# A transformer block whose pools hand out their SBUF rooms in a new order

## The chip, the cores and the metric

The kernel runs on one core of a Trainium2 chip. The metric is device time in microseconds (us) of one execution; lower is better. The program on the core is five instruction streams: TensorE (PE; its weight loads are listed apart as PEld), VectorE (DVE), ScalarE (ACT), GpSimd (POOL) and SyncE (SP). Nearly all DMAs are issued by SP, one after the other, and each stream runs in its own order and waits on semaphores for the others.

## The reference, cut to what matters

One layer on 1024 rows of width 1024, in float32: a mixer of two kinds of attention, then cross-attention to a memory of 256 rows, then a squared-ReLU MLP. The change lies in the projection ahead of the mixer.

```python
def reference(x, mem, norm1_g, w_in, ...):
    x = x + _hybrid_mixer(_rms_norm(x, norm1_g), w_in, ...)
    x = x + _memory_xattn(_rms_norm(x, norm2_g), mem, ...)
    x = x + _sq_relu_mlp(_rms_norm(x, norm3_g), w_ff_in, w_ff_out)
    return x

def _hybrid_mixer(h, w_in, ...):
    c_q, c_kv, k_idx, w_idx, q_nsa, kv_nsa, g_nsa = split(h @ w_in)     # the projection
    q_d = rope(rms_norm(rms_norm(c_q) @ w_dsa_uq))                     # 8 heads of 64
    k_d, v_d = split(rms_norm(c_kv) @ w_dsa_ukv)
    q_i = rope(rms_norm(c_q) @ w_idx_q)                                # picks 256 keys per row
    ...
    return o @ w_out                                                   # o: both attentions

def _rms_norm(x, g):
    return x * rsqrt(mean(x * x) + EPS) * g
```

## The kernel before, in words

Rows go in tiles of 128, so there are eight row tiles. `build` first runs `project(p1, 0)`, the projection of row tiles 0 to 3, on its own; its tiles live in the pool `p1`. Then `p1` is closed, and two streams run interleaved through `together`: `attend`, the attention of all row tiles (pool `aw`), and `fill`, which is `project(p2, 1)` (row tiles 4 to 7, pool `p2`), then `memory` (cross-attention's keys and values, pool `dn`), then output projections and MLP. After that a tail follows with pools of its own. PE gets dense matmuls from `fill` and many small ones from `attend`.

**Pools.** A pool hands out rooms in SBUF in the order in which its tags are first asked for; `RINGS` says how many rooms a tag has. `reuse_waits="tile"` makes a tile of a later pool wait only for the old tiles whose addresses it covers. `p2` lies where `p1` lay, and `aw` begins inside it too. Before, the order in `p2` is: `xh` (the scaled rows of the second half), `c8` (3 rooms: two for `KT`, the raw keys that `compress` reads, and one for `cq`), `c4`, `kraw`, `pc`, then the weights `wlo` and `whi`. So the second half's first weights lie on `p1`'s `whi` and `wlo`, which the last matmuls of the first half still read. The rooms `qin` and `qta` of attention's first tiles lie on `p1`'s `relu` and `c8`.

**Order.** `tc` is opened with `schedule_with_timeline_sim`: the order of each engine's stream is set by a planner which takes the waits (the rooms' too) into account, not by the order of the code alone. Moving a room can therefore move instructions.

**Names.** `weights` (L308) loads `w_in` in chunks of 256 columns, two row blocks of 128 at a time; in the second half the matmuls are plain float32 and the loads go straight into rooms called `wlo` and `whi` in turn (SP, L277), four loads to a chunk. `gemm` (L322) multiplies them; its matmuls all have line L223, as `mm` records them. `project` (L393) scales the rows (L408 in the second half, on DVE), loads eleven small vectors and tables into `pc` (L424 to L434, SP), and hands the results on: `stage_q` writes query tiles into `st` and stores them to DRAM (`q<-st`, L446). Attention reads them back (`qin<-q`, L603), turns them (L610 to L623) and transposes them on PE (`psPT<-c_ident,qd`, L629). `row_scales` (L387) makes the sums of squares of row tiles 4 to 7 (`squares` in `x4`, `relu`, then a matmul with `ones` and the square root), in the first half's `project`. In `memory`, `memT` is loaded (L908), squared on ACT (L374), reduced on DVE (L376), summed over partitions on PE (`psM<-ones,relu`) and scaled (L911).

Of the kernel before, what the change touches and what calls it, by code (L numbers as in the profile page):

```python
# [9 lines left out]
F32 = mybir.dt.float32  # L10
F32R = mybir.dt.float32r
# [11 lines left out]
P = 128  # L23
L = 1024
DM = 1024
# [9 lines left out]
NS = 4  # L35
G = 2
RINGS = {
    "p1": {"x4": 5, "st": 2, "relu": 4, "wraw": 4, "whi": 6, "wlo": 6, "c8": 4, "c4": 2, "kraw": 5, "pc": 2},
    "p2": {"x4": 5, "st": 1, "relu": 2, "whi": 4, "wlo": 4, "c8": 3, "c4": 1, "kraw": 4, "pc": 2},
    "dn": {"b4": 4, "h": 8, "relu": 2, "wraw": 2, "whi": 4, "wlo": 4},  # L40
    "res": {"b4": 4, "g": 2},
    "d2": {"b4": 2, "h": 8, "relu": 2, "whi": 4, "wlo": 4},
# [99 lines left out]
def chain(*gens):  # L142
    for x in gens:
        yield from x


def alternate(*streams):
    streams = list(streams)
    i = 0
    while streams:  # L150
        i %= len(streams)
        w = next(streams[i], None)
        if w is None:
            streams.pop(i)
        else:
            i += 1
            yield w
# [12 lines left out]
def build(nc, tc, I, C, out):  # L170
    v, s, g, te = nc.vector, nc.scalar, nc.gpsimd, nc.tensor
    ctx = ExitStack()
    W = {n: I[n][0] for n in _INS}
# [9 lines left out]
    p1 = p1_pool.__enter__()  # L183
# [6 lines left out]
    def ring(pool, tag, shape, dt=F32):  # L190
        n = RINGS[pool.name if isinstance(pool.name, str) else "dn"][tag]
        return pool.tile(shape, dt, tag=tag, name=tag, bufs=n)
# [29 lines left out]
    def mm(o, a, b, start, stop):  # L222
        te.matmul(o, a, b, start=start, stop=stop)  # L223
# [84 lines left out]
    def weights(pool, xs, nk, wsrc, parts):  # L308

        w = sum(n for _, n in parts)  # L310
        for k0 in range(0, nk, KG):
            kn = min(KG, nk - k0)
            srcs, o = [], 0
            for c0, n in parts:
                srcs.append((lambda r, o=o, n=n: r[:, :, o:o + n],
                             wsrc[k0 * P:(k0 + kn) * P, c0:c0 + n].rearrange("(k p) n -> p k n", p=P)))
                o += n
            ws = load_w(pool, [P, kn, w], *srcs) if len(xs) == 2 else load_whole(pool, [P, kn, w], *srcs)
            for k in range(kn):
                yield [x[:, k, :] for x in ws]  # L320

    def gemm(pool, xs, nk, nt, wsrc, chunks, consume, begun=None):  # L322

        for ci, parts in enumerate(chunks):
            w = sum(n for _, n in parts)
            gr = begun if ci == 0 and begun else list(weights(pool, xs, nk, wsrc, parts))
            for t in range(nt):
                pt = pst(TAGS[pool.name][0], [P, w])
                for k in range(nk):
                    if len(xs) == 1:  # L330
                        mm(pt, xs[0](t, k), gr[k][0], k == 0, k == nk - 1)
                        continue
                    wh, wl = gr[k]
                    xh, xl = xs[0](t, k), xs[1](t, k)
                    mm(pt, xh, wh, k == 0, False)
                    mm(pt, xh, wl, False, False)
                    mm(pt, xl, wh, False, k == nk - 1)
                consume(ci, t, pt)
                yield nk * (5 - len(xs)) * w / 2400.0

    def xT(pool, nt, whole=False):

        parts = [pool.tile([P, DM // P, nt * P], F32 if whole else F32R, tag="x" + n, name="x" + n)
                 for n in ("h" if whole else "hl")]
        return (parts, [lambda t, k, x=x: x[:, k, t * P:(t + 1) * P] for x in parts],
                lambda t: [x[:, :, t * P:(t + 1) * P] for x in parts])
# [20 lines left out]
    def load_xT(T):  # L367

        late["xT"][T] = small(srow, "S", L, bufs=NS).rearrange("p (k c) -> p k c", c=P)
        return nc.sync.dma_start(late["xT"][T], I["xT"][T].rearrange("p (k c) -> p k c", c=P))  # L370
# [7 lines left out]
        mm(pt, part, ones, True, True)  # L378
        return rsqrt_of(pool, pt, DM, 1, tag, r)

    def row_scale(pool, T):

        squares = ring(pool, "x4", [P, DM // P, P])
        norm_scale(pool, late["xT"][T], squares, st["r"][:, T:T + 1], "n")
        v.tensor_scalar(st["rn"][:, T:T + 1], st["r"][:, T:T + 1], -1.0, None, op0=ALU.mult)

    def row_scales(pool):  # L387

        for T in range(4, NT):
            row_scale(pool, T)  # L390
            yield 1.0

    def project(pool, part, late, st):  # L393
        t0, nt = PARTS[part]
        whole = part > 0
        parts, xf, xt_of = xT(pool, nt, whole)
        begun = []
        if not whole:
            load_xT(0)
            ws = weights(pool, xf, DM // P, W["w_in"], [(968, 256)])  # L400
            for t in range(1, nt):
                begun += [next(ws) for _ in range(KG)]
                load_xT(t)
            begun += list(ws)
        for t in range(nt):
            raw, g1 = late["xT"][t0 + t], gT["norm1_gT"]
            if whole:
                v.tensor_tensor(xt_of(t)[0], raw, g1[:, :, None].to_broadcast([P, DM // P, P]), op=ALU.mult)  # L408
            else:
                hi, lo = xt_of(t)  # L410
                for k in range(DM // P):
                    s.activation(hi[:, k, :], raw[:, k, :], AF.Copy, scale=g1[:, k:k + 1])
                    v.scalar_tensor_tensor(lo[:, k, :], raw[:, k, :], g1[:, k:k + 1], hi[:, k, :],
                                           op0=ALU.mult, op1=ALU.subtract)
                row_scale(pool, t)
            yield 1.0
        pe = late["pe"]
        cq = [ring(pool, "c8", [P, nt, 2, P], F32 if whole else F32R) for _ in xf]
        ckv = [ring(pool, "c4", [P, nt, P], F32 if whole else F32R) for _ in xf]
        kraw = [ring(pool, "kraw", [P, 6, 64]) for t in range(nt)]  # L420
        KT = []
        pc = ring(pool, "pc", [P, 512])
        cqg, ckvg, ctab = pc[:, 0:256], pc[:, 256:384], pc[:, 384:512].rearrange("p (a d) -> p a d", d=64)
        nc.sync.dma_start(cqg, row(W["dsa_cq_g"]).to_broadcast([P, 256]))  # L424
# [65 lines left out]
        def w_in(chunks, first, begun=None):  # L490
            return gemm(pool, xf, DM // P, nt, W["w_in"], chunks,
                        lambda ci, t, pt: consume(ci + first, t, pt), begun)
# [31 lines left out]
                    tc.keep_in_program_order(load_xT(4 + u))  # L524
                yield 1.0

        KT += [ring(pool, "c8", [P, 2, nt * P + (0 if part else 16)]) for _ in range(2)]
        for kv in range(0 if part else 2):
            p3 = pe[:, kv, :].rearrange("p (a l) -> p a l", a=2)
            g.tensor_copy(KT[kv][0:64, :, nt * P:], p3[0:64])  # L530
# [4 lines left out]
        yield from (alternate if part == 0 else chain)(*pair_)  # L535
        yield from gemm(pool, [lambda t, k, c=c: c[:, t, :] for c in ckv], 1, nt,
                        W["w_dsa_ukv"], [[(0, 128)]], consume_kv)
        yield from alternate(w_in([[(456, 256)], [(712, 256)]], 2), k_prep())
        ups = chain(*[gemm(pool, [lambda t, k, c=c: c[:, t, k, :] for c in cq], 2, nt,
                           W[name], [[(0, 256)], [(256, 256)]],  # L540
                           lambda ci, t, pt, k=k: stage_q(k, ci, t, pt)) for k, name in ((0, "w_dsa_uq"), (2, "w_idx_q"))])
        yield from ups if whole else alternate(ups, row_scales(pool))

    def compress(pool, part, KT, pe, st, ctab):
        t0, nt = PARTS[part]
# [803 lines left out]
```

## Time and profile before

| | us |
|---|---|
| median of 3 runs | 1786.45 (1784.96 to 1792.77) |
| the profiled execution, its time | 1783.33 |
| its span, first to last instruction | 1781.6 |

| engine | busy share of the span |
|---|---|
| PE | 94% |
| PEld | 81% |
| DVE | 57% |
| ACT | 56% |
| POOL | 50% |

The span is the execution's own time but for 1.7 us around it. The granted TensorE clock was 0.984 of full speed in the mean; it falls to one half in ten stretches of a few microseconds. In the rows further down, "idle before" with an arrow names what ended an engine's idle time; SP rows give the time that SP spent on issuing a DMA, not the transfer.

### The profile page before, as it was taken

The page shows a single profiled execution, that of the slowest core. Times are in us where ns is not written, and L with a number is a line of the kernel's source. Part 1 is how long each engine was busy: PE and PEld are TensorE (multiplying, and loading weights), DVE is VectorE, ACT ScalarE, POOL GpSimd, SP SyncE. Part 2 cuts the span into 40 slices and gives each one's busy share as a digit, 9 for nine tenths or more (in the row PEclk, how much of TensorE's full clock was granted, in tenths as well). Part 3 has the DMA queues.
Part 4 walks back from the last instruction along what each step waited for, and adds up shares of the span by engine and source line. Part 5 has one row for each costly group of instructions (what it writes and reads, how often), then busy time and mean ns, then how long its engine had stood idle before and what let it go on. Part 6 is the DMA issues. An engine that isn't in the chain of part 4 may idle for free.

```text
span 1781.6 us, 27924 instructions
## 1 busy us (share of the span) xinstructions
PE 1682.7 (94%) x9266; PEld 1446.4 (81%) x9266; DVE 1018.8 (57%) x2843; ACT 991.8 (56%) x2319; POOL 884.6 (50%) x1025
## 2 busy tenths in 40 slices
PE   6987998899999999999999999999989889999998
PEld 6986987778888878788878888787878778888887
DVE  6575788775786796566665576735325452222223
ACT  6543775764686679556865589554214443333333
POOL 2354556554542447676566675563002354444445
PEclk9998999999999999999999999999989999999999
DMA  6424221555354321212222212125574443333333
GB/s 190 122 102 125 72 57 69 174 135 160 92 148 127 100 59 59 82 56 70 64 65 66 69 55 72 57 72 167 182 228 130 130 130 95 95 95 95 95 118 107
DMA packets 172944, 186.45 MB, mean 105 GB/s; under 512 B 25472, under 2 KB 141952, under 8 KB 172800
## 3 DMA queue, kind: packets, MB, share of 16 engines
q1 hardware_dynamic: 164864, 174.18, 32.1%
q0 software_dynamic: 7936, 10.49, 2.2%
q8 instruction: 73, 1.20, 0.3%
q14 instruction: 71, 0.58, 0.1%
HBM read 166.80 MB, written 17.83 MB: 104 GB/s over the span
## 4 chain that ended last, share of the span: by engine, by line
PE 53%; DVE 6%; ACT 3%; DMA 2%; POOL 2%; issue 2%; SPq 1%; POOLq 0%; ACTq 0%; DVEq 0%
PE psD L223 40%; PE psS L223 7%; PE psPV L223 3%; PE psPT L744 2%; ACT dmask L685 1%; POOL wlo L261 1%; DVE pl L245 1%; DMA wraw<-in_w_ff_in_dram 1%; DMA whi<-in_w_out_dram 1%; ACT S L729 1%; DVE S L727 1%; DVE tkj L686 1%; PE psM L290 0%; POOL S L734 0%; DVE b L943 0%
## 5 line engine op out<-in xcount | busy, mean ns | idle before, releaser
L261 POOL TENSOR_TENSOR wlo<-wraw,whi 128x512 fp32r<-128x512 f32 (+1 forms) x225 | 303.9, 1356 | 286.1 <-ACT whi L256 279.1
L223 PE MATMUL psD<-whi,h 128*128 128x512 f32 x1024 | 342.6, 401 | 12.0 <-DVE b L943 5.5
L256 ACT ACTIVATE whi<-wraw 128x512 fp32r<-128x512 f32 x321 | 200.3, 627 | 213.1 <-PE psD L223 159.6
L223 PEld LDWEIGHTS psD<-whi,h 128*128 128x128 f32 x1024 | 193.1, 190 | 55.8 <-DVE b L1201 8.8
L223 PE MATMUL psD<-xh,whi 128*128 128x512 f32 (+1 forms) x576 | 212.5, 372 | 1.6 <-ACT xh L244 1.6
L223 PE MATMUL psD<-xh,wlo 128*128 128x512 f32 (+1 forms) x576 | 211.7, 369 | 0.0
L223 PE MATMUL psD<-xl,whi 128*128 128x512 f32 (+1 forms) x576 | 210.5, 369 | 0.0
L223 PE MATMUL psD<-wlo,h 128*128 128x512 f32 x512 | 203.4, 398 | 0.1
L223 PE MATMUL psD<-wlo,xh 128*128 128x256 f32 (+1 forms) x608 | 169.4, 353 | 13.8 <-DMA wlo<-in_w_in_dram 11.3
L729 ACT ACTIVATE S<-S,mn 128x128 f32<-128x128 f32 (+7 forms) x192 | 143.1, 746 | 66.2 <-DVE mn L727 65.3
L223 PE MATMUL psD<-whi,xh 128*128 128x256 f32 (+1 forms) x608 | 165.7, 351 | 11.3 <-ACT whi L256 10.3
L245 DVE TENSOR_TENSOR pl<-psPT,ph 128x512 fp32r<-128x512 f32 (+1 forms) x232 | 141.7, 618 | 49.1 <-ACT ph L244 48.5
L244 ACT ACTIVATE ph<-psPT 128x512 fp32r<-128x512 f32 (+1 forms) x232 | 122.3, 540 | 77.9 <-PE psPT L744 62.9
L261 DVE TENSOR_TENSOR wlo<-wraw,whi 128x512 fp32r<-128x512 f32 (+1 forms) x96 | 78.4, 816 | 150.5 <-ACT whi L256 150.4
L734 POOL TENSOR_SCALAR S<-S,sums,gi 128x640 f32<-128x640 f32 (+7 forms) x128 | 111.5, 882 | 77.0 <-DVE sums L732 71.2
L744 PE MATMUL psPT<-c_ident,S 128*128 128x128 f32 x816 | 131.5, 276 | 5.2 <-POOL S L734 3.3
L223 PEld LDWEIGHTS psD<-wlo,xh 128*128 128x128 f32 x608 | 116.9, 198 | 22.8 <-issue 11.4
L223 PEld LDWEIGHTS psD<-whi,xh 128*128 128x128 f32 x608 | 115.3, 196 | 19.8 <-ACT whi L256 10.3
L223 PEld LDWEIGHTS psD<-xh,whi 128*128 128x128 f32 x576 | 108.0, 188 | 18.3 <-ACT xh L244 2.1
L223 PEld LDWEIGHTS psD<-xl,whi 128*128 128x128 f32 x576 | 108.2, 188 | 17.1
L223 PEld LDWEIGHTS psD<-xh,wlo 128*128 128x128 f32 x576 | 108.2, 188 | 16.8
L223 PE MATMUL psS<-K,qh 128*128 128x384 f32 (+3 forms) x288 | 111.0, 388 | 5.1 <-DVE mn L727 2.6
(304 smaller groups left out, 3910.1 us busy)
## 6 DMA issues: line engine op xcount, KB each, us to landing
wraw<-in_w_ff_in_dram SPq DMA_DIRECT2D x40, 512.0 KB, 4.0
wraw<-in_w_ff_out_dram SPq DMA_DIRECT2D x40, 512.0 KB, 3.9
wraw<-in_w_ff_in_dram SPq DMA_DIRECT2D x64, 256.0 KB, 2.7
wraw<-in_w_ff_out_dram SPq DMA_DIRECT2D x64, 256.0 KB, 2.6
whi<-in_w_out_dram SPq DMA_DIRECT2D x32, 256.0 KB, 4.0
wlo<-in_w_out_dram SPq DMA_DIRECT2D x32, 256.0 KB, 4.0
wraw<-in_w_in_dram SPq DMA_DIRECT2D x24, 256.0 KB, 3.6
q<-st SPq DMA_DIRECT2D x12, 512.0 KB, 2.7
```

What stands on the lines that cost most here:

```text
L223: te.matmul(o, a, b, start=start, stop=stop)
L244: s.activation(hi, src, AF.Copy)
L245: v.tensor_tensor(lo, src, hi, op=ALU.subtract)
L256: s.activation(hi, raw, AF.Copy)
L261: (v if l == "v" else g).tensor_tensor(lo, raw, hi, op=ALU.subtract)
L685: s.activation(mask, src, AF.Sign, bias=tks[:, i, 1:2], accum_out=over[:, 0:1])
L686: v.scalar_tensor_tensor(small(aw, "tkj", 3), over, nd, tks[:, i, :], op0=ALU.is_gt, op1=ALU.mult, accum_out=tks[:, i + 1, 1:2] if b else ...
L727: v.tensor_tensor_reduce(out=dst, in0=sp, in1=m, scale=1.0, scalar=mn[:, 0:1] if i else 3e38, op0=ALU.add, op1=ALU.min, accum_out=low)
L729: s.activation(S, S, AF.Exp, bias=low, scale=-1.0, accum_out=sums[:, hh:hh + 1])
L734: g.tensor_scalar(Ss[hh], Ss[hh], sums[:, hh:hh + 1], 1.0 if gate is None else gate[:, hh:hh + 1], op0=ALU.mult, op1=ALU.mult)
L744: te.transpose(p2[:, j, hh, :], S[:, (c + j) * P:(c + j + 1) * P], ident)
```

## The change

`c8` is split into the tags `kt` and `cq`. `project` asks for its rooms in another order: `xh` first, then, in the second half, the four loads of the first weights, then `kt`; in the first half `wraw`, `whi` and `wlo` next, then `cq`, the squares and `c4`, and `xl` only then. So in `p2` the first weights `wlo` and `whi` now lie behind `xh`, on what were `p1`'s `kt` and `wraw`; `aw`'s first rooms lie on `p1`'s `xl`. `row_scale` can be given its room for the squares. The sums of squares of row tiles 4 to 7 stand in the code beside the second chunk of `w_in`'s query columns, where they stood beside the query up-projections. No instruction is added or removed: SP, PE, DVE, ACT and POOL have as many of each form as before.

```diff
-    "p1": {"x4": 5, "st": 2, "relu": 4, "wraw": 4, "whi": 6, "wlo": 6, "c8": 4, "c4": 2, "kraw": 5, "pc": 2},
-    "p2": {"x4": 5, "st": 1, "relu": 2, "whi": 4, "wlo": 4, "c8": 3, "c4": 1, "kraw": 4, "pc": 2},
+    "p1": {"x4": 5, "st": 2, "relu": 4, "wraw": 4, "whi": 6, "wlo": 6, "kt": 2, "cq": 2, "c4": 2, "kraw": 5, "pc": 2},
+    "p2": {"x4": 5, "st": 1, "relu": 2, "whi": 4, "wlo": 4, "kt": 2, "cq": 1, "c4": 1, "kraw": 4, "pc": 2},
...
-    def row_scale(pool, T):
+    def row_scale(pool, T, squares=None):
-        squares = ring(pool, "x4", [P, DM // P, P])
+        squares = ring(pool, "x4", [P, DM // P, P]) if squares is None else squares
...
-        parts, xf, xt_of = xT(pool, nt, whole)
-        begun = []
+        nx = 1 if whole else 2
+        first = pool.tile([P, DM // P, nt * P], F32 if whole else F32R, tag="xh", name="xh")
+        if whole:
+            begun = list(weights(pool, [first], DM // P, W["w_in"], [(968, 256)]))
+        KT = [ring(pool, "kt", [P, 2, nt * P + (0 if part else 16)]) for _ in range(2)]
         if not whole:
+            begun = []
             load_xT(0)
-            ws = weights(pool, xf, DM // P, W["w_in"], [(968, 256)])
+            ws = weights(pool, [first, first], DM // P, W["w_in"], [(968, 256)])
...
+        cq = [ring(pool, "cq", [P, nt, 2, P], F32 if whole else F32R) for _ in range(nx)]
+        squares = None if whole else ring(pool, "x4", [P, DM // P, P])
+        ckv = [ring(pool, "c4", [P, nt, P], F32 if whole else F32R) for _ in range(nx)]
+        parts = [first] + [pool.tile([P, DM // P, nt * P], F32R, tag="xl", name="xl") for _ in range(nx - 1)]
...
-        KT += [ring(pool, "c8", [P, 2, nt * P + (0 if part else 16)]) for _ in range(2)]
...
-        yield from alternate(w_in([[(456, 256)], [(712, 256)]], 2), k_prep())
-        ups = chain(*[gemm(...) for k, name in ((0, "w_dsa_uq"), (2, "w_idx_q"))])
-        yield from ups if whole else alternate(ups, row_scales(pool))
+        yield from alternate(w_in([[(456, 256)], [(712, 256)]], 2), k_prep() if whole else chain(k_prep(), row_scales(pool)))
+        yield from chain(*[gemm(...) for k, name in ((0, "w_dsa_uq"), (2, "w_idx_q"))])
```

The streams of before and after are the same up to the end of the first half, on every engine. The first place where they part is SP, behind the last store of the first half's queries. Before (`pc` are the small vectors, `qin` the first query tile that attention reads back, `wlo` and `whi` the second half's first weights):

```order
L446 DMA q201_89<-st_1882 128x1024
L603 DMA qin_1922<-q100_84 128x256
L424 DMA pc_2061<-in_dsa_cq_g_dram 128x256
L425 DMA pc_2061<-in_dsa_ckv_g_dram 128x128
L426 DMA pc_2061<-in_c_ccos_dram 128x64
L427 DMA pc_2061<-in_c_csin_dram 128x64
L434 DMA pc_2068<-in_nsa_kn_g_dram 128x64 x4
L434 DMA pc_2068<-in_dsa_kn_g_dram 128x64
L434 DMA pc_2068<-in_idx_k_ln_g_dram 128x64
L434 DMA pc_2068<-in_idx_k_ln_b_dram 128x64
L277 DMA wlo_2078<-in_w_in_dram 128x2x256
L277 DMA whi_2080<-in_w_in_dram 128x2x256
```

After, on SP behind the same store:

```order
L457 DMA q201_89<-st_1882 128x1024
L277 DMA wlo_1921<-in_w_in_dram 128x2x256
L277 DMA whi_1923<-in_w_in_dram 128x2x256
L277 DMA wlo_1925<-in_w_in_dram 128x2x256
L277 DMA whi_1927<-in_w_in_dram 128x2x256
L612 DMA qin_1934<-q100_84 128x256
L435 DMA pc_2071<-in_dsa_cq_g_dram 128x256
L436 DMA pc_2071<-in_dsa_ckv_g_dram 128x128
L437 DMA pc_2071<-in_c_ccos_dram 128x64
```

The four weight loads now stand ahead of `qin` and the eleven loads of `pc`, where they stood behind them.

PE at the same handover, before (the `psM` row is the last matmul of the first half, `psD<-..,xh` are the second half's, `psPT<-c_ident,qd` are attention's first transposes):

```order
L223 MATMUL psM_1783<-ones_76,relu_1781 128x1
L223 MATMUL psD_2086<-wlo_2078,xh_1920 128x256 x2
L223 MATMUL psD_2193<-wlo_2078,xh_1920 128x256 x2
L223 MATMUL psD_2086<-whi_2080,xh_1920 128x256 x2
L223 MATMUL psD_2193<-whi_2080,xh_1920 128x256 x2
L629 MATMUL psPT_1943<-c_ident_360,qd_1938 128x128 x4
L223 MATMUL psD_2086<-wlo_2082,xh_1920 128x256 x2
```

PE at the same place, after:

```order
L223 MATMUL psM_1743<-ones_76,relu_1741 128x1
L223 MATMUL psD_2086<-wlo_1921,xh_1920 128x256 x2
L223 MATMUL psD_2193<-wlo_1921,xh_1920 128x256 x2
L223 MATMUL psD_2086<-whi_1923,xh_1920 128x256 x2
L223 MATMUL psD_2193<-whi_1923,xh_1920 128x256 x2
L223 MATMUL psD_2086<-wlo_1925,xh_1920 128x256 x2
L223 MATMUL psD_2193<-wlo_1925,xh_1920 128x256 x2
L223 MATMUL psD_2086<-whi_1927,xh_1920 128x256 x2
L223 MATMUL psD_2193<-whi_1927,xh_1920 128x256 x2
L638 MATMUL psPT_1955<-c_ident_366,qd_1950 128x128 x4
```

Attention's first transposes stand behind sixteen matmuls of the second half, where they stood behind eight.

The second place is SP where `memory` begins, before (`q241` is the last store of the second half's queries, `o12` and `o13` are stores of attention's results, `h` and `b4` are `memory`'s tiles, `w_xk` its first weights):

```order
L446 DMA q241_91<-st_5089 128x1024
L758 DMA o12_102<-oc_3986 64x2x128
L903 DMA h_5169<-in_xk_norm_g_dram 128x128
L908 DMA b4_5172<-in_memT_dram 128x1024
L908 DMA b4_5215<-in_memT_dram 128x1024
L758 DMA o13_103<-oc_4079 64x2x128
L277 DMA whi_5237<-in_w_xk_dram 128x2x256
```

After, on SP at the same place:

```order
L767 DMA o11_101<-oc_3887 64x2x128
L912 DMA h_5169<-in_xk_norm_g_dram 128x128
L917 DMA b4_5172<-in_memT_dram 128x1024
L917 DMA b4_5215<-in_memT_dram 128x1024
L612 DMA qin_4840<-q001_81 128x256
L277 DMA whi_5237<-in_w_xk_dram 128x2x256
```

The loads of `memT` stand behind the store of `o11`, where they stood behind that of `o12`; on PE 46 matmuls of attention now stand between the second half's last matmul and `memory`'s first one, where 38 stood. From there on single instructions trade places, by some tens of rows at most, until both streams agree again in the tail.

## Rows read from the trace of the kernel before

**Rows 1.** The page's head: busy us of an engine, share, instructions.

```profile
PE 1682.7 (94%) x9266; PEld 1446.4 (81%) x9266; DVE 1018.8 (57%) x2843; ACT 991.8 (56%) x2319; POOL 884.6 (50%) x1025
```

**Rows 2.** Busy time by stretches: us, busy us (instructions) of each engine, clock, DMA.

```profile
132.60:142.90 10.30, 0.00 (x0) 0.00 (x0) 6.48 (x13) 0.42 (x1) 6.20 (x10) 0.50 0.61 166
142.90:146.30 3.40, 3.36 (x8) 2.77 (x9) 0.30 (x1) 0.00 (x0) 0.59 (x3) 0.50 1.07 374
...
340.80:347.70 6.90, 6.35 (x17) 4.99 (x18) 6.90 (x16) 3.08 (x10) 2.35 (x4) 0.51 0.75 230
```

The five busy times are PE, PEld, DVE, ACT and POOL; then come PE's granted clock, the busy share of the DMA engines, and GB/s.

**Rows 3.** The timeline of PE at the handover: start, us, instruction, idle before.

```profile
131.34 0.28 PE L223 MATMUL psM<-ones,relu 128*128 128x1 f32 x2
142.94 3.62 PE L223 MATMUL psD<-wlo,xh 128*128 128x256 f32 x8 [11.32 <-DMA wlo<-in_w_in_dram]
146.39 1.89 PE L223 MATMUL psD<-whi,xh 128*128 128x256 f32 x8
148.12 0.60 PE L629 MATMUL psPT<-c_ident,qd 128*128 128x128 f32 x4
```

**Rows 4.** The timeline of SP's DMA issues in the same stretch.

```profile
115.09 17.26 SPq L446 DMA_DIRECT2D q<-st  x5
132.52 0.32 SPq L603 DMA_DIRECT2D qin<-q  x1
...
138.51 0.43 SPq L277 DMA_DIRECT2D wlo<-in_w_in_dram  x1
...
140.96 0.46 SPq L277 DMA_DIRECT2D wlo<-in_w_in_dram  x1
```

**Rows 5.** DMAs issued from 132.0 to 139.2: KB each, us from issue to landing.

```profile
q<-st SPq DMA_DIRECT2D x1, 512.0 KB, 2.9
wlo<-in_w_in_dram SPq DMA_DIRECT2D x1, 256.0 KB, 4.3
qin<-q SPq DMA_DIRECT2D x1, 128.0 KB, 3.3
...
pc<-in_c_ccos_dram SPq DMA_DIRECT2D x1, 32.0 KB, 3.5
```

**Rows 6.** The timeline of DVE, ACT and POOL at the handover.

```profile
133.28 4.79 DVE L408 TENSOR_TENSOR xh<-S,norm_gT 128x1024 f32<-128x1024 f32 x4
...
135.89 0.42 ACT L613 ACTIVATE qta<-qin 128x256 f32<-128x256 f32 x1 [3.97 <-DVE xh L408]
...
138.01 0.41 DVE L615 TENSOR_REDUCE qss<-qta 128x4 f32<-128x256 f32 x1
...
140.62 0.43 DVE L620 TENSOR_TENSOR qtb<-qin,qtab 128x256 f32<-128x256 f32 x1 [1.94 <-POOL qin L618]
...
141.71 0.96 POOL L623 TENSOR_TENSOR qd<-qta,qtb 128x256 f32<-128x256 f32 x1
```

**Rows 7.** The timeline of the second handover, where `memory` begins, over the engines.

```profile
328.11 1.03 PE L223 MATMUL psD<-wlo,c 128*128 128x256 f32 x4
...
330.28 0.58 SPq L758 DMA_DIRECT2D o<-oc  x1
...
331.57 0.91 SPq L908 DMA_DIRECT2D b<-in_memT_dram  x2
...
337.62 1.06 ACT L374 ACTIVATE xh<-b 128x1024 f32<-128x1024 f32 x1 [2.30 <-DMA b<-in_memT_dram]
...
338.71 1.91 DVE L376 TENSOR_REDUCE relu<-xh 128x128 f32<-128x1024 f32 x1 [2.71 <-ACT xh L374]
...
340.68 0.45 PE L223 MATMUL psM<-ones,relu 128*128 128x1 f32 x2 [3.80 <-DVE relu L376]
```

**Rows 8.** Busy time from the first handover to the second, columns as in rows 2.

```profile
143.00:350.00 207.00, 194.21 (x1076) 167.51 (x1077) 152.87 (x560) 139.08 (x455) 114.44 (x184) 0.98 0.32 94
```

**Rows 9.** PE's clock around another long wait, columns as in rows 2.

```profile
1291.70:1297.10 5.40, 0.00 (x0) 0.00 (x0) 1.19 (x5) 2.30 (x8) 1.83 (x4) 0.64 1.05 297
1297.20:1303.40 6.20, 6.20 (x15) 4.96 (x16) 0.00 (x0) 0.00 (x0) 0.00 (x0) 0.50 1.12 362
```

More of the change, by code (lines that the diff above doesn't have):

```diff
@@ L404, in project, with xt_of @@
             begun += list(ws)
+        cq = [ring(pool, "cq", [P, nt, 2, P], F32 if whole else F32R) for _ in range(nx)]
+        squares = None if whole else ring(pool, "x4", [P, DM // P, P])
+        ckv = [ring(pool, "c4", [P, nt, P], F32 if whole else F32R) for _ in range(nx)]
+        parts = [first] + [pool.tile([P, DM // P, nt * P], F32R, tag="xl", name="xl") for _ in range(nx - 1)]
+        xf = [lambda t, k, x=x: x[:, k, t * P:(t + 1) * P] for x in parts]
+        def xt_of(t):
+            return [x[:, :, t * P:(t + 1) * P] for x in parts]
         for t in range(nt):
@@ L414, in project @@
                                            op0=ALU.mult, op1=ALU.subtract)
-                row_scale(pool, t)
+                row_scale(pool, t, squares)
+                squares = None
             yield 1.0
         pe = late["pe"]
-        cq = [ring(pool, "c8", [P, nt, 2, P], F32 if whole else F32R) for _ in xf]
-        ckv = [ring(pool, "c4", [P, nt, P], F32 if whole else F32R) for _ in xf]
         kraw = [ring(pool, "kraw", [P, 6, 64]) for t in range(nt)]
-        KT = []
         pc = ring(pool, "pc", [P, 512])
@@ L537, in project @@
                         W["w_dsa_ukv"], [[(0, 128)]], consume_kv)
-        yield from alternate(w_in([[(456, 256)], [(712, 256)]], 2), k_prep())
-        ups = chain(*[gemm(pool, [lambda t, k, c=c: c[:, t, k, :] for c in cq], 2, nt,
+        yield from alternate(w_in([[(456, 256)], [(712, 256)]], 2), k_prep() if whole else chain(k_prep(), row_scales(pool)))
+        yield from chain(*[gemm(pool, [lambda t, k, c=c: c[:, t, k, :] for c in cq], 2, nt,
                            W[name], [[(0, 256)], [(256, 256)]],
                            lambda ci, t, pt, k=k: stage_q(k, ci, t, pt)) for k, name in ((0, "w_dsa_uq"), (2, "w_idx_q"))])
-        yield from ups if whole else alternate(ups, row_scales(pool))
     def compress(pool, part, KT, pe, st, ctab):
```

## The prediction

> **What bounds the kernel now.** I began with the page's head: PE is busy for 94% of the span, twice the others [rows 1]. So what counts is the idle time of PE, about 95 us in all (the span less PE's busy time), and any stretch at half clock. The list of waits then gives the longest single wait of PE behind the start-up: 11.32 us between the last matmul of the first half, which ends at 131.62, and the first of the second half at 142.94 [rows 3]. It ends with the landing of the second half's first weights. PE does nothing in it, and the clock falls to one half about a microsecond in; it stays there until 146.3, 3.35 us behind the restart [rows 2].
>
> Why do the weights come so late? SP issues the last store of queries near 132.0, then one `qin` at 132.52, then eleven loads of `pc`, and only at 138.51 the first weight load, which lands 4.3 us later [rows 4, 5]. The weights' old room, on the first half's `whi`, was free at 131.6. So by 138.51 it is no longer the room that holds them: it is their place in SP's stream. The other operand is earlier: `xh`, four DVE operations of 1.2 us from 133.28, of which the first two row tiles are done by 135.7 [rows 6].
>
> **The change part by part.** *Weights ahead of `qin` and `pc`.* With rooms that are free from the middle of the first half, the four loads stand directly behind the last store, in `qin`'s old place, so the first is issued at 132.52. Its landing was not seen there. Nearest rows: `qin`, from the same place behind the same store, 3.3 us, but with half the bytes; the same weight load in a crowd of small ones, 4.3; the 512 KB store itself, 2.9 [rows 5]. So 135.4 at the earliest, 136.8 at the latest. The early end is cut by `xh`, whose second row tile (135.7) is wanted by PE's third matmul. I take 136.1, near to `qin`, plus some tenths for the second half of the bytes. **Gain: 142.94 less 136.1 = 6.8 us** (6.1 to 7.4).
>
> The rule of the Trainium skill, DMA: Bandwidth & Descriptors, section "Anatomy of one DMA", is a fixed 2.0 us plus the bytes at 436 GB/s; it is stated for GpSimd's path, not SP's. By it 256 KB would take 2.6 us (an estimate), the weights would be there at 135.1, and `xh` alone would set the restart, for a gain near 7.3. The rows of this place (2.9 to 4.3 us) are all above it, so the sum does not use it.
>
> *The clock.* PE still idles for 4.5 us. The fall came about 1 us after the last matmul, so it is not avoided. Before, the first 3.35 us after the restart ran at half clock [rows 2]; I take the same, at no difference. The bound: behind the 5.5 us wait near 1291.7 half clock held for 6.2 us of work [rows 9]; 2.9 us more of that at half speed would cost 1.4 us. The other way, if the clock came back at once, 1.7 us would be gained.
>
> *`qin` behind the weights.* It is issued four weight issues later, by the spacing of the five at 138.51 to 140.96 at 134.97, 2.45 us later [rows 4], and lands at 138.3 (3.3) or 139.3 (4.3). Then ACT makes `qta` (0.42), DVE `qss` (0.41). Before, `qss` ran at 138.01, not when `qta` was ready (136.31) but when `xh` left DVE [rows 6]; this slack hides 1.7 of the 2.45. So `qss` runs at 138.7 and `qd` is ready at 143.4 instead of 142.67, or at 144.4. PE asks for it only behind sixteen of the program's matmuls. The trace counts each of these as two: before, the first eight counts lasted from 142.94 to 146.39 at half clock, the next eight from there to 148.12 at full clock [rows 3]. So 3.45 us and then three times 1.73: 136.1 + 8.6 = 144.7. No new wait; 0.3 us of cover at the bad end. If it opens, it costs tenths.
>
> *`pc` behind both.* Eleven loads go back by 2.45 us. Two operations on tables in `pc` stand on DVE ahead of `qtb` (140.62). Each SP load here also waits until the eighth DMA before it has landed, so the last table is issued when the first weights are in, near 136.1, and lands 3.5 us later [rows 5], at 139.6; `qtb` wants DVE at 141.3. Hidden, with 1.7 us of cover. The next chunk of weights is issued behind them near 140 and lands by 145; PE wants it behind 24 more matmuls, after 150.
>
> *What attention gets.* Its first transposes come at 144.7 instead of 148.12: 3.4 us earlier, not 6.8, as eight matmuls of the second half have gone ahead of them. That is an exchange of work, no loss, as long as PE is the bound. From 143 to 350 PE is busy for 194.2 of 207 us and DVE and ACT for 153 and 139 [rows 8], so a lag of 3.4 us should mostly drown.
>
> *The second handover.* PE waits 3.80 us for `memory`'s first matmul, which waits for DVE, ACT and the load of `memT` in turn [rows 7]; half clock until 347.7 follows, with 6.35 us of work that would take half of that [rows 2], so this place costs 3.8 + 3.2 = 7.0 us in all. Before: from the end of the second half's last matmul (329.14) to the first of `memory` (340.68) it is 11.5 us, and PE has 7.7 us of attention for them. After: the `memT` loads stand behind the store of `o11`. Its value is made behind ten attention matmuls that follow the last projection matmul (2 us), one ACT and one DVE step (1.2); then the store and one load (1.2), 6.0 us to land, 1.06 on ACT, 1.91 on DVE: 13.4 us. PE's cover is 46 matmuls instead of 38, 9.3 us. The wait is 4.1 instead of 3.8: the same, at a net of -0.3.
>
> *Rooms of attention's first tiles* cost and bring nothing: `qin` waits by its place on SP, not by its room. *Sums of squares:* in all five streams they stand where they stood, the order being the planner's, so nothing comes sooner: 0. *The rest:* small trades of place, with no instruction more; 0, with 1.5 us to either side, as all waits of PE between 143 and 350 sum to 12.8 us.
>
> **Sum:** 6.8 - 0.3 = 6.5 us. In terms of the profiled execution: 1783.33 - 6.5 = 1776.8. That execution was 3.1 us below the median of the three, so against the median: 1786.45 - 6.5 = **1780**.
>
> **The rivals.** *Second handover healed.* If `memT` lands before PE has run out of attention, 3.8 us and most of the 3.2 us of clock go too: 1780 - 7 = 1773. For it: the loads now hang on an earlier store. Against: that store follows the last projection matmul as closely as the old one did. 15%.
>
> *Gain given back.* Attention gains only 3.4 us, and if its ACT and DVE chain sets when `memT`'s store and `memory` can begin, PE meets that wait 3.4 us earlier than it ends, and longer half clock takes a part of the rest: 1783 to 1787, say 1785. For it: the wait at 340.68 was set by a load, not by PE. Against: PE is busy for 94% of the stretch between [rows 8]. This includes that the change does not do what it says, with the first weights slow behind the 512 KB store. 22%.
>
> The same page of the Trainium skill, section "Queues, rings and completion order", says that each DMA engine takes a queue's descriptors in ring order. By it the weights move only behind the store's bytes; what that costs is in `qin`'s 3.3 us, which came behind the same store.
>
> *Slower.* One mechanism: the fill runs dry. The second half's last matmuls now go out ahead of attention by some thirty places, so PE has attention alone until `memory` starts, at the speed of its ACT and DVE chain. The wait there decides: it must grow from 3.8 to over 10.6 us to eat the 6.8, and half clock then adds 1.7. At 13 us it is 1786.45 - 6.8 + 9.2 + 1.7 = 1790.5. Against: 46 matmuls still stand between. 6%.
>
> **How the numbers follow.** Forecast 57%, at 1780, its own range 1777 to 1783 (the landing, clock and small trades above). Healed 15% (1773), given back 22% (1785), slower 6% (1790.5). The range that leaves out 2 in 10: 1772 to 1787; it cuts off the slower case, part of the healed one and the far ends. What a measurement of this kernel can tell from no change is about 0.5%, 8.9 us: faster than 1777.5 is the healed case plus a good tenth of the forecast; slower than 1795.4 only the far end of the slower case. So faster 0.24, same 0.71, slower 0.05.
>
> **What would show it.** In the profile after: the first weight issue near 132.5; PE's wait there 4.5 us (3.8 to 5.2), ended by the weights' DMA or by `xh`; half clock until about 139.5; first `qd` transposes near 144.7 without a wait ahead of them; the wait ahead of `psM<-ones,relu` 3 to 5 us near 334. The forecast is wrong if that last wait is gone or has doubled, if PE waits for `qd` or the second chunk of weights, or if the waits between 143 and 350 have grown from 12.8 us by over 3.

## The result and the profile after

The changed kernel takes 1802.4 us (median of 9 runs, 1794.62 to 1808.52) against 1786.45 for the kernel before. The ratio is **1.0085, 95% interval 1.0064 to 1.0106**: slower by 15 us, where 1780 was forecast with a range up to 1787. The profiled execution of after took 1794.7 us (span 1792.9) at a mean granted clock of 0.984, that of before's profile.

The page's head of after, in the columns of [rows 1]:

```profile
PE 1689.6 (94%) x9266; PEld 1449.1 (81%) x9266; DVE 1030.3 (57%) x2843; ACT 992.6 (55%) x2319; POOL 885.9 (49%) x1025
```

PE is busy for 6.9 us more, with no instruction more, and its idle time (span less busy) grows from 98.9 to 103.3 us, although the wait that the change was aimed at has shrunk as forecast. PE's timeline at the first handover, against [rows 3]:

```profile
130.64 0.28 PE L223 MATMUL psM<-ones,relu 128*128 128x1 f32 x2
135.37 3.75 PE L223 MATMUL psD<-wlo,xh 128*128 128x256 f32 x8 [4.45 <-DMA wlo<-in_w_in_dram]
138.92 2.80 PE L223 MATMUL psD<-whi,xh 128*128 128x256 f32 x8
141.56 1.89 PE L223 MATMUL psD<-wlo,xh 128*128 128x256 f32 x8
143.28 1.89 PE L223 MATMUL psD<-whi,xh 128*128 128x256 f32 x8
145.01 0.60 PE L638 MATMUL psPT<-c_ident,qd 128*128 128x128 f32 x4
```

The 11.32 us have become 4.45, and the transposes follow at 145.01 with no wait ahead of them. On SP the first weight load is issued at 131.74, in `qin`'s old place, against [rows 4]:

```profile
131.74 0.39 SPq L277 DMA_DIRECT2D wlo<-in_w_in_dram  x1
...
134.19 0.42 SPq L612 DMA_DIRECT2D qin<-q  x1
```

The stretches behind the two handovers and between them, in the columns of [rows 2]:

```profile
135.40:140.70 5.30, 5.30 (x13) 4.22 (x14) 2.67 (x7) 0.42 (x1) 1.41 (x3) 0.50 0.65 197
...
332.90:338.70 5.80, 5.80 (x16) 4.53 (x17) 5.80 (x14) 2.48 (x7) 0.56 (x1) 0.50 0.86 268
```
```profile
143.00:350.00 207.00, 193.88 (x1082) 166.35 (x1081) 153.75 (x563) 138.58 (x454) 114.07 (x188) 0.98 0.33 101
```

Half clock (0.50, the lower of the two levels) follows both, as before. From 143 to 350 PE's busy time is what it was [rows 8], but the two windows do not hold the same work: that of before has 3.3 us more at half clock in it, behind its later restart. The second handover on PE, against [rows 7]:

```profile
332.87 0.58 PE L223 MATMUL psM<-ones,relu 128*128 128x1 f32 x2 [4.28 <-DVE relu L376]
```

So both places came out as forecast, and the loss is elsewhere. To find it I counted PE's matmul records in order and noted when each count is reached, at places in the program where both orders have done the same work. Us later (+) or earlier (-) than before:

| before's time | 143 | 330 | 400 | 463 | 542 | 630 | 686 | 770 | 1107 | 1154 | end |
|---|---|---|---|---|---|---|---|---|---|---|---|
| after | -7.6 | -3.6 | -4.0 | -2.8 | +0.6 | +3.0 | +5.4 | +7.6 | +8.2 | +10.4 | +11.4 |

The profiles of all kernels in this document lie between 1.3 us ahead of before and 0.7 behind at 130 us, up to where they run one order, so a difference of about 1 us says nothing. The lead falls by half before the second handover, holds until 400, and then some 12 us are lost by 770 and 2 more near 1150. No single wait does that. PE's waits from 150 to 1285, before and after (what PE waited for: us in total, times, longest):

```profile
PE psPV L223 <- DVE pl L245: 7.9, 14, 2.1
PE psD L223 <- DVE b L943: 5.5, 4, 1.7
...
PE psS L223 <- DVE mn L727: 3.2, 8, 0.7
...
PE psPV L223 <- ACT ph L244: 1.9, 2, 1.6
```
```profile
PE psS L223 <- DVE mn L736: 10.6, 12, 2.3
PE psPV L223 <- DVE pl L245: 6.1, 11, 1.2
...
PE psPV L223 <- ACT ph L244: 4.0, 6, 1.1
PE psS L223 <- ACT ir L660: 3.5, 4, 1.4
...
PE psPV L223 <- DVE oc L766: 2.7, 3, 1.1
PE psD L223 <- DMA b<-o: 2.4, 2, 1.5
```

Some went (`b`), more came: many waits of 0.3 to 2.3 us, on DVE and ACT results of attention and on the loads `b<-o`. What one of them looks like: PE, and then DVE, in after near 493 us (`psD<-h` 128x128 is a result of cross-attention, twelve matmuls, here the last ten).

```profile
488.19 1.31 PE L223 MATMUL psD<-h 128*128 128x128 f32 x10
...
493.18 1.13 PE L223 MATMUL psD<-whi,b 128*128 128x256 f32 x4 [1.24 <-DVE relu L1038]
```
```profile
491.25 0.81 DVE L675 SCALAR_TENSOR_TENSOR tkh<-dmask,isc 128x640 int16<-128x640 int16 x1
491.98 0.81 DVE L676 TENSOR_TENSOR tkl<-isc,dmask 128x640 int16<-128x640 int16 x1
492.72 0.41 DVE L1038 TENSOR_TENSOR relu<-psD,xsum 128x256 f32<-128x256 f32 x1
```

The same step in before, near 500 us:

```profile
496.47 0.45 PE L223 MATMUL psD<-h 128*128 128x128 f32 x3
...
500.20 1.05 PE L223 MATMUL psD<-whi,b 128*128 128x256 f32 x4
```
```profile
498.92 0.81 DVE L667 TENSOR_TENSOR tkl<-isc,dmask 128x640 int16<-128x640 int16 x1
499.66 0.41 DVE L1029 TENSOR_TENSOR relu<-psD,xsum 128x256 f32<-128x256 f32 x1
```

`relu` (the fill's) must have read this `psD` before PE's matmuls `psD<-whi,b` write into its room; `psD` has two. DVE does not pause in either kernel, and in both `tkh` and `tkl`, steps of attention's top-k search, stand ahead of `relu`. Neither row runs slower: `tkl` takes 0.81 us and `relu` 0.41 in both. (All DVE rows together are busy for 11.5 us more by the two heads, over many rows; that was not taken apart.) What differs is what stands between on the two engines. In after the last `psD<-h` ends at 489.50, PE is through its other matmuls 2.45 us later, and `relu` is done 3.6 us later (493.13): PE waits. In before it ends at 496.92, PE is through its other matmuls 3.3 us later, and `relu` is done 3.15 us later (500.07): PE does not wait. So 0.8 us less cover on PE and 0.5 us more ahead of `relu` on DVE make this wait.

### The profile page after: what moved, and what is told of

Its sections match the earlier page's. It is cut to its first block, busy times and chain, and to the rows that moved or that the text cites. A ratio compares the mean times of both kernels' runs of the same rounds, so it can differ in the third digit from the quotient of the medians.

```text
span 1792.9 us, 27919 instructions
## 1 busy us (share of the span) xinstructions
PE 1689.6 (94%) x9266; PEld 1449.1 (81%) x9266; DVE 1030.3 (57%) x2843; ACT 992.6 (55%) x2319; POOL 885.9 (49%) x1025
## 4 chain that ended last, share of the span: by engine, by line
PE 61%; DVE 14%; ACT 7%; POOL 4%; issue 4%; DMA 4%; SPq 0%; POOLq 0%; DVEq 0%; ACTq 0%
PE psD L223 44%; PE psS L223 8%; PE psPV L223 4%; PE psPT L753 3%; ACT dmask L694 3%; DVE pl L245 1%; DMA qin<-q 1%; DVE S L736 1%; DVE tkj L695 1%; ACT S L738 1%; DVE isc L666 1%; ACT ph L244 1%; POOL S L743 1%; ACT whi L256 1%; DMA whi<-in_w_out_dram 1%
## 5 line engine op out<-in xcount | busy, mean ns | idle before, releaser
L223 PE MATMUL psD<-whi,xh 128*128 128x256 f32 (+1 forms) x608 | 166.5, 352 | 12.8 <-ACT whi L256 11.1
L743 POOL TENSOR_SCALAR S<-S,sums,gi 128x640 f32<-128x640 f32 (+7 forms) x128 | 106.6, 844 | 81.1 <-DVE sums L741 73.3
L223 PE MATMUL psS<-K,qh 128*128 128x384 f32 (+3 forms) x288 | 112.0, 392 | 10.1 <-DVE mn L736 8.4
```

What stands on the lines that cost most here:

```text
L743: g.tensor_scalar(Ss[hh], Ss[hh], sums[:, hh:hh + 1], 1.0 if gate is None else gate[:, hh:hh + 1], op0=ALU.mult, op1=ALU.mult)
```

## The experiments

**What the order hangs on.** Parts of the change, each put into the kernel alone, show which of them moves instructions. Before with the later sums of squares alone has the order of before on all five engines; after without them has the order of after. New rooms in `p1` alone: the order of before. New rooms in `p2` alone: the order of after. So it is the second half's room order, with its first weights on rooms that are free early, that makes the planner draw the rest anew (their loads also stand earlier in the code; the two were not taken apart). Each instruction moves by some tens of rows at most, but over half of them move: at 4739 of PE's 8390 places another instruction stands, and at 1788 of DVE's 2609.

The runs therefore separate rooms from order. Nine of the twelve kernels hold PE, DVE, ACT and POOL to an order written down, by an edge from each instruction to the next that sets the order alone and adds no wait; SP stays the planner's. The edit is always this; eight of the nine have the rooms of after without the moved sums, which move nothing, the ninth those of before, and otherwise only the table `ORDER` differs:

```diff
         build(nc, tc, I, C, out)
+        in_order(nc, tc)
...
+def in_order(nc, tc):
+    traced = nc.cur_bb.bb.instructions
+    for rows in json.loads(zlib.decompress(base64.b85decode(ORDER))).values():
+        for x, y in zip(rows, rows[1:]):
+            tc.add_manual_dep(traced[y], traced[x].name,
+                              mybir.DependencyInfo(mybir.DependencyClass.NoSync, mybir.DependencyReason.DATA),
+                              reason="order")
```

My theory when I began was the reordering; the rival, that the new rooms themselves cost time.

**Rooms of after, order of before.** Expected:

> The changed kernel's rooms (sums of squares in their old place in the code, which alters no instruction's order), with PE, DVE, ACT and POOL held to the order of before, instruction for instruction; SP is free and puts the four weight loads ahead of qin as in the changed kernel. Theory 'order': the 16 us lost are the re-drawn order of the middle of the program, so they are gone; the wait at the first handover shrinks from 11.3 to 4.5 us, and PE then waits some 2.5 us for qd, as the transposes stand behind eight matmuls only: about 4 us under before, 1779 to 1784. Theory 'rooms': new neighbours in SBUF or the later qin cost time in the middle whatever the order: 1795 or more.

Measured 1785.16 us, ratio 0.9988 (0.9967 to 1.001). The loss is gone, so the rooms do not cause it. But most of the gain is gone too: about 2 us under before, within the interval, where 1779 to 1784 was expected. PE there:

```profile
136.74 3.75 PE L223 MATMUL psD<-wlo,xh 128*128 128x256 f32 x8 [4.61 <-DMA wlo<-in_w_in_dram]
140.29 2.86 PE L223 MATMUL psD<-whi,xh 128*128 128x256 f32 x8
144.27 0.66 PE L639 MATMUL psPT<-c_ident,qd 128*128 128x128 f32 x4 [1.13 <-POOL qd L633]
...
152.86 1.11 PE L490 MATMUL psM<-c_ident,relu 128*128 128x128 f32 x4 [3.06 <-ACT relu L486]
```

The old order asks for `qd` behind eight of the program's matmuls instead of sixteen, and meets waits of 1.13 and 3.06 us and a second stretch of half clock. A lead of 6.2 us at 143 is 0.7 behind at 330, and stays within 1 us of before until 1230. To this order, drawn for late weights, early ones are worth next to nothing.

**Rooms of before, order of after.** Expected:

> The rooms of before, with PE, DVE, ACT and POOL held to the order of the changed kernel; SP is free and issues the first weights last, as before. Theory 'order': the loss of the middle comes without the gain of the handover: 1802 + 7 = 1806 to 1812. Theory 'rooms': near before, 1784 to 1790.

Measured 1809.35 us, ratio 1.0127 (1.0112 to 1.0142), as theory 'order' said, with the first wait back:

```profile
142.46 3.75 PE L223 MATMUL psD<-wlo,xh 128*128 128x256 f32 x8 [11.88 <-DMA wlo<-in_w_in_dram]
```

With the four corners filled, by ratios times 1786: order of before, old rooms 0 and new rooms -2; order of after, old rooms +23 and new rooms +15. The order costs 17 to 23 us; the rooms save 2 to 8, of which the 2 is not clear of noise.

**Other drawings.** Three kernels add one such edge to the planner's graph and let it draw everything else anew. In the first, on after, the first weight load stands behind `qin`. Its edit, and that of the other two but for the pair of numbers:

```diff
+        traced = nc.cur_bb.bb.instructions
+        for later, first in [(1417, 1422)]:
+            tc.add_manual_dep(traced[later], traced[first].name,
+                              mybir.DependencyInfo(mybir.DependencyClass.NoSync, mybir.DependencyReason.DATA),
+                              reason="order")
```

> The changed kernel with one edge more: its first weight load is issued behind qin, not ahead of it; the planner then draws the order anew from there (some 4200 of 8390 places on PE differ from the changed kernel, 1640 from before). Theory 'order' gives no value of its own, only that it can lie anywhere between 1775 and 1805, and nearer to before than to the changed kernel as its order is nearer: 1778 to 1790. Theory 'lag' (attention starts too late against the fill): with qin 2.5 us earlier most of the 16 us are gone, 1779 to 1786.

Measured 1787.83 us, ratio 1.0014 (0.9999 to 1.0029). Its order differs from after's at 4217 of PE's places and from before's at 1638. PE's wait at the handover is 6.59 us; a lead of 5.6 us behind it is 3.6 at 200 and gone by 600. Most of the loss is gone, as theory 'lag' said too, but the run does not test that theory: two of the four loads, `whi`, are still ahead of `qin`, `qin` is issued 1.2 us earlier than in after (132.96 against 134.19), not 2.5, and half of the order is another. In the second, on before, attention's first transposes stand behind sixteen matmuls (2629 of PE's places differ); in the third, on before, `qin` stands behind all loads of `pc` (827 differ):

> The kernel before with one edge more: attention's first transposes stand behind sixteen matmuls of the second half instead of eight, as in the changed kernel; rooms and the 11.3 us wait at the handover stay. The planner draws the order anew from there (2630 of 8390 places on PE differ from before). Theory 'order': a re-drawn order alone moves the time by several us, in either direction: outside 1784 to 1790. Theory 'rooms': within 2 us of before.

Measured 1789.97 us, ratio 1.002 (1.0002 to 1.0038): inside 1784 to 1790, so theory 'order' misses, and 2.4 us over the median of before's 25 runs beside it, so theory 'rooms' misses too, barely.

> The rooms of before, with one edge more in the planner's graph that puts the first qin behind the last load of pc on SP; 827 of PE's 8390 places differ from before, all by the planner's redrawing. Theory (each drawing has a time of its own, some us to either side, whatever the edge itself costs): qin's own cost is hidden, and the time comes out 1782 to 1795. Rival (the planner's drawing does not matter, only the edge does, and attention's first tile comes 3 us later): 1786 to 1789.

Measured 1786.07 us, ratio 0.9998 (0.9981 to 1.0014), inside both ranges, so it does not choose between them. A new drawing need not cost 15 us: these three lie within 0.2% of before, and after's own is the slow one among four.

**Which part of the new order.** The first cut was near 380 us, rooms of after in all that follows:

> Rooms of the changed kernel; PE, DVE, ACT and POOL hold the changed kernel's order up to about 380 us and the order of before from there on (both orders have done the same work by then). At the points where both orders have done the same PE work, the changed kernel's trace is 7.6 us ahead of before at 143 us, 4.9 ahead at 378, and 11.3 behind at the end. Theory 'order': the lead of 378 is kept, as all behind it is as before: about 5 us under before, ratio 0.9965 to 0.9985. Rival 'a lead cannot be kept' (whoever reaches the middle early waits there for attention's ACT and DVE chain, in any order): no faster than before, ratio 0.999 or more.

Measured 1790.97 us, ratio 1.0031 (1.0011 to 1.005), a miss, and one of my making: the cut lay at 381 us on PE and at 396 on DVE. At the seam PE waits 2.62 and 2.94 us, and its clock is at one half from 381.4 to 398.5:

```profile
385.92 0.58 PE L223 MATMUL psPV<-pl,V 128*128 128x256 f32 x1 [2.62 <-DVE tkc L709]
...
391.49 0.69 PE L223 MATMUL psS<-K,qh 128*128 128x384 f32 x1 [2.94 <-DVE mn L737]
```

Nine us go there, from 1.9 ahead to 7.1 behind; from 400 to 1107 the lag stays at 7.1, so the order of before keeps what it is given. The mirror, and a cut near 770:

> The mirror: rooms of the changed kernel, order of before up to about 380 us, the changed kernel's order from there on. Theory 'order': before's time at 378 (new rooms in the old order had no lead left by then) plus the 16.2 us that the changed kernel's trace loses from 378 to the end: 1800 to 1806, ratio about 1.009. Rival: with no lead to give back, near before, 1785 to 1790.

> As the first of these, with the cut at 770 us, where the changed kernel's trace stands 7.6 us behind before. Theory 'order', with the loss spread over the middle: 1793 to 1797, ratio about 1.004; it tells whether the loss lies ahead of 770 or behind. If it lies behind only: 1783.

Measured 1808.38 us, ratio 1.0125 (1.0095 to 1.0155), above the 1800 to 1806 expected, and 1791.98, ratio 1.0041 (1.002 to 1.0063). The mirror has the same bad seam (7.7 us) and loses 21 more from 400 on. The third, at the ratio expected, loses 14 us between 425 and 770, with the order of after, and from there on, with that of before, none: it regains 6. That pointed to the stretch from 400 to 770, but two of the three carry a seam. So the cuts were set at 400, where those of the four engines lie within 3.5 us, and at 793:

> Rooms of after; all of PE, DVE, ACT and POOL are held to the order of after up to places that run near 400 us (PE 400.6, DVE 400.0, ACT 401.9, POOL 403.5), and to the order of before from there on. In new_order_to_380 the cuts of the engines lay 15 us apart and 9 us were lost at the seam. Theory (the order of after is the better one up to 400, by about 4 us, and loses only later; the order of before keeps any lead): no wait at the seam, 4 us ahead of before at 400 and 3 to 5 at the end, 1781 to 1784, ratio 0.997 to 0.999. Rival (the lead at 400 is work put off, and the order of before has to catch it up): the lead is gone by 600 and the time is 1786 to 1791.

> The mirror: rooms of after, the order of before up to near 400 us and the order of after from there on. Theory (the later order of after loses by itself, whatever came before it): like before up to 400, then 13 to 19 us lost up to the end, 1799 to 1805, ratio 1.007 to 1.010. Rival (the later order of after loses only because its earlier part put attention behind): 1785 to 1790.

> Rooms of after; PE, DVE, ACT and POOL are held to the order of before, but between places that run near 400 and near 793 us they are held to the order of after. Theory (the order of after loses in this stretch by itself: PE's busy time between 460 and 780 falls from 308 to 301 us): 7 to 9 us later at 793, held to the end, 1792 to 1796, ratio 1.004 to 1.006. Rival (what is lost there is work that stands earlier, and the order of before catches it up further on): 1784 to 1788.

> The mirror: the order of after, but the order of before between 400 and 793 us. Theory (half of the loss and more lies in that stretch): PE busy near 308 us between 460 and 780, 3 us ahead at 793, then 4 us lost near 1150, 1786 to 1791, ratio 1.001 to 1.003. Rival (the loss is spread evenly, or later stretches lose what this one saves): 1795 to 1803.

| order of after in | us | ratio (95%) | PE ahead (-) or behind (+) at 463 | 542 | 770 | 1107 | 1154 | end |
|---|---|---|---|---|---|---|---|---|
| nowhere | 1785.16 | 0.9988 (0.9967, 1.001) | +0.9 | 0 | -0.1 | 0 | 0 | +2.1 |
| 0 to 400 | 1786.46 | 1.0004 (0.9988, 1.002) | -2.7 | -2.8 | -3.1 | -2.9 | -2.9 | +3.5 |
| 400 to 793 | 1793.25 | 1.005 (1.0033, 1.0067) | 0 | +3.1 | +9.0 | +7.8 | +7.8 | +10.1 |
| 400 to the end | 1801.25 | 1.0084 (1.0058, 1.011) | -0.2 | +3.2 | +9.4 | +11.6 | +15.1 | +20.6 |
| all but 400 to 793 | 1794.17 | 1.0057 (1.0036, 1.0078) | -0.2 | -0.5 | -0.6 | +2.9 | +5.9 | +7.7 |
| everywhere | 1802.4 | 1.0085 (1.0064, 1.0106) | -2.8 | +0.6 | +7.6 | +8.2 | +10.4 | +11.4 |

The stretch from 400 to 793 alone costs 0.62% (1.005 against 0.9988), about 11 us (8 to 9 by the two traces), as theory said, and its rival (caught up later) falls: the 7.8 us are still there at 1154. The order of after from 400 on loses as much behind an unchanged beginning as theory said (1801.25), so the rival (it loses only because its earlier part put attention behind) falls, and theory 'lag' with it. One line tells each kernel apart, the busy time from 460 to 780 us (PE first). With the order of before there: before, rooms of after alone, and new up to 400:

```profile
460.00:780.00 320.00, 307.69 (x1769) 262.86 (x1770) 235.07 (x731) 228.52 (x542) 166.54 (x207) 1.00 0.31 91
```
```profile
460.00:780.00 320.00, 308.54 (x1774) 264.51 (x1773) 234.77 (x737) 229.27 (x545) 166.91 (x207) 0.99 0.31 91
```
```profile
460.00:780.00 320.00, 308.31 (x1771) 263.43 (x1770) 235.44 (x731) 227.37 (x539) 166.72 (x207) 1.00 0.31 93
```

With the order of after there: after, new from 400 to the end, and new from 400 to 793 alone:

```profile
460.00:780.00 320.00, 300.83 (x1719) 258.21 (x1719) 232.40 (x716) 224.25 (x528) 161.90 (x201) 0.99 0.30 91
```
```profile
460.00:780.00 320.00, 300.73 (x1727) 258.75 (x1728) 233.07 (x718) 225.64 (x535) 161.99 (x202) 0.99 0.30 91
```
```profile
460.00:780.00 320.00, 301.17 (x1731) 259.03 (x1730) 233.32 (x718) 226.14 (x537) 162.76 (x203) 0.99 0.29 91
```

307.7 to 308.5 with the one order, 300.7 to 301.2 with the other, whatever stands ahead. PE's waits from 460 to 800 in before, and then in the last of these kernels (new from 400 to 793):

```profile
PE psPV L223 <- DVE pl L245: 2.5, 8, 0.5
...
PE psS L223 <- DVE mn L727: 0.9, 2, 0.6
...
PE psS L223 <- ACT ir L651: 0.3, 1, 0.3
```

```profile
PE psPV L223 <- DVE pl L245: 3.4, 6, 1.0
PE psS L223 <- ACT ir L661: 2.3, 3, 1.4
PE psS L223 <- DVE mn L737: 2.0, 4, 0.6
...
PE psD L223 <- DVE relu L1039: 1.2, 1, 1.2
```

In after the same four are 2.7, 2.3, 2.0 and 1.2 us. In all six kernels with the order of after in this stretch, one of them on the rooms of before, those on `ir`, `mn` and `relu` are 2.3, 1.9 to 2.0 and 1.2 us; in the five with the order of before 0.3, 0.9 and none. The wait on `relu` is that of 1.24 us shown above, at the same size:

```profile
495.99 1.13 PE L223 MATMUL psD<-whi,b 128*128 128x256 f32 x4 [1.24 <-DVE relu L1039]
```

Waits are not all of it. Between 400 and 793 PE's idle time grows from 13.0 us in before to 20.4 in after, at the same work (396 to 799 of its own time), and after has 6.8 us at half clock there (from 659.6 and from 731.3), nearly all with PE at work, where before has none; that is 3.3 us more. The other kernels with the order of after there have 6.8 to 10.2 us of half clock, the others with that of before none or 3.4.

*Two misses.* Order of after up to 400 alone did not come out at 1781 to 1784. Its lead of 2.9 us, of which 1.2 was there at 60 us, ahead of any difference in order, is kept within 0.4 us from 463 to 1232, so the rival (work put off) falls as well; it is lost at the weight loads of `w_out` and behind them. PE in that kernel, and then in before (the second wait of before is the one in [rows 9]):

```profile
1240.44 3.75 PE L223 MATMUL psD<-whi,b 128*128 128x256 f32 x8 [3.12 <-DMA whi<-in_w_out_dram]
...
1298.64 2.93 PE L223 MATMUL psS<-whi,b 128*128 128x256 f32 x6 [7.22 <-DMA whi<-in_w_out_dram]
```
```profile
1241.79 3.58 PE L223 MATMUL psD<-whi,b 128*128 128x256 f32 x8 [1.58 <-DMA whi<-in_w_out_dram]
...
1297.19 3.78 PE L223 MATMUL psS<-whi,b 128*128 128x256 f32 x8 [5.49 <-DMA whi<-in_w_out_dram]
```

The first load is issued 2.57 us earlier than in before (1233.86 against 1236.43, SP's issues) and PE goes on only 1.35 us earlier; behind the second, issued at the same time (1291.30 against 1291.36), PE goes on 1.45 us later. That is a gain given back to transfers, 1000 us behind the place where it was made. And all but 400 to 793 was expected at 1786 to 1791 and took 1794.17. The stretch itself did as expected (0.6 us ahead at 770), but the order behind it costs more than I read from after: 3.5 us from 770 to 1107 and 3.0 more by 1154, where after lost 0.6 and 2.2. From the ratios of the kernels with and without it (1.0084 against 1.005, 1.0057 against 1.0004), the order of after behind 793 costs 6 to 10 us; it was not taken apart further.

No kernel here beats before by more than the measurement can tell; the best ratio is 0.9988.

## Why the prediction was wrong

**First handover: right, but for the clock.** The gain of 6.8 us was built from an issue at 132.5, a wait of 4.5, half clock until about 139.5, `qd`'s transposes at 144.7 without a wait. The trace has 131.74, 4.45, 140.75 and 145.01. The clock's term, put at no difference, was mis-sized: half clock lasted 5.4 us behind the restart, not 3.35, and the second eight counts took 2.64 us, not 1.73, which is 0.9 us, inside the bound of 1.4. The lead at 143 is 7.6 us, of which 0.7 was there from 60 us on, so 6.9. The steps behind `qin` hold as well: `qss` runs at 138.62 and `qtb` at 141.24, where 138.7 and 141.3 were forecast, and nothing waits for them. From the issue at 131.74 to PE's restart at 135.37 are 3.6 us, inside the 2.9 to 4.3 that the rows gave. By the rule of the Trainium skill, DMA: Bandwidth & Descriptors, section "Anatomy of one DMA", it would have been 2.6 us (the prediction's estimate, for a path other than SP's); the trace does not agree.

**Second handover: right.** 4.28 us measured, 4.1 forecast; neither healed nor run dry.

**What attention gets: half wrong.** "A lag of 3.4 us should mostly drown" did not hold in full: the lead was 3.6 us at 330, not 6.5. That is the rival "gain given back", in its first part; 0.9 us of it is the clock's term above, the rest was not taken apart.

**The rest: this step failed.** "Small trades of place, with no instruction more; 0, with 1.5 us to either side." Its bound came from PE's waits between 143 and 350, and PE's idle time in that window did hardly change (12.8 us before, 13.1 after). But the trades of place reach to 1426 us of before's trace and move over half of PE's instructions; from 400 to 793 they cost 11 us, and behind that 6 to 10 more. They were priced by their first 200 us. The sign that I named (waits grown by over 3 us) was to be looked for in the same stretch, so it did not show either.

**The slower rival** had a price and a place, the second handover, and neither was it. What was slower was no single wait, but many small ones: from 150 to 1285 those on `mn` grew from 3.2 us (8 times) to 10.6 (12 times), those on `ph` from 1.9 to 4.0, and those on `ir`, `oc` and `b<-o` came up to 3.5, 2.7 and 2.4. **Sums of squares, 0:** right, shown by the orders.

**The clock's part.** Runs of one mean granted clock lie nearly as far apart as the medians. At 0.984 after took 1794.6 and 1794.7 us, and three of the 23 runs of before that go with the cuts at 400 took 1778.9 to 1783.8; at 0.978 and 0.979 five runs of after took 1801.4 to 1808.5, and five of before (one of those 23, four of the 25 that go with the first experiments) 1788.2 to 1793.4. That is some 13 us at either clock, where the medians are 16 apart. But the mean does not tell what PE did at half clock. The two profiles have 58 us of it each; in before PE works in 41.5 of these, as most of the long first wait lies in the rest, in after in 50.0. So of the 11.3 us between the two spans, 4.4 are idle time, 4.3 are work that now runs at half speed (half of the 8.5 us), and 2.6 are left over. After also has the lower mean more often, 0.979 in its median against 0.981 to 0.982; why was not shown.

*Still open:* why the planner's drawing for these rooms is worse on the chip than before's. The runs show which stretch, and that the waits there are on results of DVE and ACT and come with the order. As the held kernels exchange the order of all four engines together, they do not show whose order makes the waits, nor which single trade costs how much.

## What to carry to other kernels

Where a planner or scheduler sets the order, a moved room is not a local change: compare the two orders over the whole program first, and if they differ widely, give "the rest" a range as wide as other drawings show, here 0 to +0.9%, not one read from the stretch around the change. To learn what the change itself is worth, hold the old order on the new rooms and the new order on the old ones; the four corners tell rooms from order. A lead won early can be lost late: the one kept here to 1232 us went at the next weight loads.

## What the runs showed of the hardware

Small waits came back with the order: 1.24 us on `relu` in after was 1.24 in another kernel, with another order ahead of it, and 1.2 in all six kernels that have this order there. What half clock cost hung on whether PE worked in it: two profiles with 58 us of it each differ by 8.5 us of work at half speed. The spread between runs of one kernel, ten us and more, goes in good part with its mean granted clock: of those 23 runs of before, three at 0.984 took 1778.9 to 1783.8 us and two at 0.980 1788.1 and 1788.7, nearly 2 us for each 0.001 (a line through all 23 gives 2.2, through the 25 of the first experiments 1.6). And the same load of `w_out`, issued 2.57 us earlier, took 1.2 us longer (6.6 against 5.4 from issue to PE's restart).
